# PE order of the paired projections written out, decays loaded behind a part's first level, one tile for three weight sums

## The chip, the cores and the metric

The kernel runs on one core of one Trainium2 chip. The metric is the time of one execution on the device in microseconds (us). The core's engines work in parallel, each through a queue of its own in program order: TensorE (PE, matrix products; PEld are its weight loads), VectorE (DVE), ScalarE (ACT), GpSimd (POOL), and SyncE (SP), which here issues DMA transfers. Semaphores hold an instruction back until what it reads, or what it overwrites, is ready.

## The reference, cut to what matters

128 context tokens and 1024 latent tokens, 1152 in all, go through one layer with D = 1024. The normalised and modulated input h is projected by one weight w_in, and the parts of the projection take different ways:

```python
proj = h @ w_in
q, ff, fb, vi, zA, u, zB, gA, gB = split(proj)
qh = silu(heads(q))                                # 8 heads of 128
log_f, k = forget_gate(ff, lb)                     # f = lb + (1-lb)*sigmoid(ff), k = 1 - f; fb likewise
S_t = diag(f_t) S_(t-1) + k_t v_t^T                # forward in time, and backward with fb
o_t = S_t^T q_t
yA = rms_norm(o_f + o_b) * gnorm_w * silu(zA)
yB = real(fft2(u)) * silu(zB)                      # 4 groups of 128 channels
merged = sigmoid(gA) * (yA @ w_pa) + sigmoid(gB) * (yB @ w_pb)
out = merged @ w_o                                 # then a residual and a norm
```

## The kernel before

The kernel goes through stages: normalisation and the projection of v (to 171 us in the profiled execution), the paired projections (171 to 874 us), the scan of the heads with the branch products (from 874 us) and the output products at the end.

**The paired projections.** `pair(n, evacs)` (L622) projects two column blocks of w_in, 256 columns, for all 1152 tokens by a seven-product scheme (one Strassen step). `PRODUCTS = (1, 5, 6, 2, 7, 4, 3)` is the order of the products. Each has two halves j of 288 tokens, and `mm3` (L205 to L211) makes 12 matmuls of 128x288 of a half: 4 k blocks by 3 terms, since each weight and each input is held as hi + lo (hi*hi L209, lo*hi by L210, hi*lo by L211). So a product has 24 matmuls. Each product has its weights: `raw` (1 MB, two DMAs of 512 KB, L626, one buffer) holds the pair's four blocks; weights 1, 2 and 4 are a block itself, 5, 6 and 3 are sums s1, s2, s2, and 7 is a difference made in raw (L636 on DVE). `split` (L616) makes hi by an ACT cast (L618, wh) and lo by a subtraction (L619, wl: on POOL for 1, 2 and 4, on DVE for the others). Five buffers of hi and lo go round. Products add up in PSUM banks: ACT copies the sums in between to x (L646), DVE or ACT makes the result c (L656, L654), `done` (L659) runs the output's function (silu, sigmoid, forget gate, or nothing) and stores it (L661). Pairs 1 and 2 make u, 3 to 18 the eight heads' q, f, f backward and gate, 19 to 23 the gates, 24 and 25 zB, 26 and 27 gates again.

**Side work.** A generator `four` is stepped from `pair` after some products: first the Fourier transform of u (`fourier`), then `pieces` (L561), which prepares the scan's heads in 16 parts (8 heads, of 640 and 512 tokens each). A part loads its decays f (tile px, L571) and queries q (tile pz, L574), makes kk = 1 - f (ACT, L585, two), qq = q*f (DVE, L586, two) and k0 = the sum of both kk (DVE, L587). Three levels follow, each with 20 or 16 groups of small matmuls 32x32 (`within`, L484), a `merge` into the scores (L475, L477), and, between levels, two ACT copies of halves into the matmuls' operands k0 and q (L470) and a growth of kk, qq and f by the decays (`grow`, DVE, L464 and L466). Behind the second growth it copies f for later (L599), asks for the next part's f (L571), stores kk, qq, f (L602 to L604), and behind the third level asks for the next part's q (L574).

**What sets the order.** A scheduler orders each engine's instructions before the run. Two instructions keep the order in which they are written only where one depends on the other. The helper `matmul` (L201) adds such a dependency between a matmul and the one written before it. The scan stage uses it; the matmuls of `pair` and `within` are plain, so there the scheduler places the levels between a pair's matmuls.

**The start of the scan.** `load_head` (L447) loads a head's kk, qq (1.2 MB each) and fa back. Head 0's loads are made ahead of the last gates, those of heads 1 and 2 at the stage's end.

## Time and profile before

| | us |
|---|---|
| median of 3 runs (lowest, highest) | 1337.24 (1336.79, 1341.56) |
| the profiled execution: its time | 1345.96 |
| the profiled execution: span of the trace | 1344.2 |
| PE busy in the span | 1260.1 (94%) |
| DVE busy | 836.3 (62%) |
| ACT busy | 628.7 (47%) |
| POOL busy | 479.4 (36%) |

The span runs from the first to the last instruction of the trace; the execution's own time is 1.8 us longer. Busy shares are averages over all stages. PE leads by far, so the places count where PE stands still, and the stretches in which the clock granted to it (PEclk, as a share of 2.4 GHz) falls to 0.50, which is 1.2 GHz. A wait is put down to the instruction that released it; "issue" is a wait whose releaser the profile doesn't show.

### The profile page before, as it was taken

How to read it: one execution, taken by the hardware profiler on the slowest of the kernel's cores; microseconds unless marked ns; L12 is line 12 of the kernel's file. 1: busy time of each engine (PE TensorE's matmuls, PEld its weight loads, DVE VectorE, ACT ScalarE, POOL GpSimd, SP SyncE). 2: the span in 40 equal slices, each digit the busy share in tenths (PEclk: the TensorE clock that was granted, in tenths of full speed). 3: DMA queues.
4: the chain of work that ended last, by engine and by line, in shares of the span. 5: the costliest groups of instructions: out<-in, count | busy, mean ns of one | idle time of the engine just before them, and what ended most of it. 6: DMA issues, size and time to landing. Idle time of an engine off the chain costs nothing.

```text
span 1344.2 us, 31219 instructions
## 1 busy us (share of the span) xinstructions
PE 1260.1 (94%) x12768; PEld 1183.8 (88%) x12768; DVE 836.3 (62%) x1391; ACT 628.7 (47%) x1290; POOL 479.4 (36%) x359
## 2 busy tenths in 40 slices
PE   5999989999999989999999999988999889999998
PEld 3679989999998889898899999977899788999886
DVE  7737743434356676675777444485988788565554
ACT  5542233454455655656556444453555444332332
POOL 4515523324412212222112128221432455564563
PEclk7799989999999989999999999998999889999999
DMA  8542223434445546446555634664667754676332
GB/s 314 211 169 65 79 98 116 133 105 149 150 137 183 191 141 230 138 161 204 187 195 186 221 120 153 219 211 153 243 228 237 230 173 131 192 224 211 131 128 95
DMA packets 126162, 229.88 MB, mean 171 GB/s; under 512 B 11441, under 2 KB 78786, under 8 KB 121794
## 3 DMA queue, kind: packets, MB, share of 16 engines
q1 hardware_dynamic: 125730, 226.83, 50.1%
q8 instruction: 100, 1.64, 0.5%
q10 hardware_dynamic: 288, 1.05, 0.3%
q14 instruction: 44, 0.36, 0.1%
HBM read 154.82 MB, written 73.02 MB: 170 GB/s over the span
## 4 chain that ended last, share of the span: by engine, by line
PE 50%; DMA 12%; DVE 10%; issue 5%; ACT 3%; POOL 2%; SPq 1%; DVEq 0%; POOLq 0%; ACTq 0%
PE o_ps L210 7%; PE o_ps L209 7%; PE o_ps L211 7%; PE d_ps L209 5%; PE d_ps L211 5%; PE d_ps L210 5%; DMA raw<-in_w_pr 4%; PE d_ps L200 4%; PE o_ps L200 3%; DMA ya_dr<-gz 2%; DMA wr<-in_w_o 2%; DMA px<-f_dr 1%; PE s_ps L547 1%; DMA yr<-ya_dr 1%; PE s_ps L200 1%
## 5 line engine op out<-in xcount | busy, mean ns | idle before, releaser
L619 POOL TENSOR_TENSOR wl<-raw,wh 128x512 fp32r<-128x512 f32 x81 | 119.5, 1476 | 444.5 <-ACT wh L618 422.3
L619 DVE TENSOR_TENSOR wl<-s,wh 128x512 fp32r<-128x512 f32 x81 | 60.8, 755 | 80.9 <-ACT wh L618 80.7
L186 POOL TENSOR_TENSOR w_lo<-w_raw,w_hi 128x512 fp32r<-128x512 f32 (+1 forms) x36 | 65.0, 1808 | 121.8 <-ACT w_hi L184 121.8
L618 ACT CAST wh<-raw 128x512 fp32r<-128x512 f32 x108 | 66.3, 615 | 71.1 <-DMA raw<-in_w_pr 34.6
L211 PE MATMUL o_ps<-h1h,wl 128*128 128x288 f32 x324 | 98.3, 303 | 0.2 <-POOL wl L619 0.2
L209 PE MATMUL o_ps<-h1h,wh 128*128 128x288 f32 x324 | 97.7, 301 | 0.7 <-ACT wh L618 0.6
L210 PE MATMUL o_ps<-h1l,wh 128*128 128x288 f32 x324 | 97.9, 302 | 0.0
L200 PE MATMUL d_ps<-yh,w_hi 128*128 128x288 f32 x256 | 82.2, 321 | 10.5 <-ACT w_hi L184 5.7
L618 ACT CAST wh<-s 128x512 fp32r<-128x512 f32 x81 | 50.2, 620 | 88.7 <-DVE s L636 26.7
L930 POOL TENSOR_TENSOR merged<-merged,gs 128x288 f32<-128x288 f32 x64 | 64.4, 1018 | 62.5 <-DVE gs L929 59.2
L200 PE MATMUL d_ps<-yh,w_lo 128*128 128x288 f32 x256 | 77.8, 304 | 3.6 <-POOL w_lo L186 3.6
L656 DVE TENSOR_TENSOR c<-o_ps,x 128x288 f32<-128x288 f32 x108 | 47.8, 450 | 53.1 <-PE o_ps L211 43.2
L200 PE MATMUL d_ps<-yl,w_hi 128*128 128x288 f32 x256 | 77.2, 302 | 0.0
L464 DVE TENSOR_TENSOR kk<-kk,fa 128x1152 f32<-128x1152 f32 x40 | 58.9, 1476 | 14.9 <-PE s_ps L200 8.6
L464 DVE TENSOR_TENSOR qq<-qq,fa 128x1152 f32<-128x1152 f32 x40 | 63.7, 1593 | 0.5
L209 PEld LDWEIGHTS o_ps<-h1h,wh 128*128 128x128 f32 x324 | 62.4, 193 | 1.2 <-ACT wh L618 0.8
L211 PEld LDWEIGHTS o_ps<-h1h,wl 128*128 128x128 f32 x324 | 62.3, 192 | 1.1 <-POOL wl L619 0.4
L210 PEld LDWEIGHTS o_ps<-h1l,wh 128*128 128x128 f32 x324 | 62.3, 192 | 0.5 <-issue 0.3
L636 DVE TENSOR_TENSOR s<-raw 128x512 f32<-128x512 f32 x27 | 27.6, 1020 | 55.6 <-DMA raw<-in_w_pr 55.6
L200 PEld LDWEIGHTS d_ps<-yh,w_hi 128*128 128x128 f32 x256 | 50.0, 195 | 12.0 <-ACT w_hi L184 6.1
L586 DVE TENSOR_TENSOR px<-pz,px 128x640 f32<-128x640 f32 (+1 forms) x32 | 23.8, 785 | 53.0 <-DMA px<-f_dr 31.7
L184 ACT CAST w_hi<-w_raw 128x512 fp32r<-128x512 f32 (+1 forms) x48 | 34.8, 725 | 40.6 <-DMA w_raw<-in_w_pab 10.5
(386 smaller groups left out, 4662.9 us busy)
## 6 DMA issues: line engine op xcount, KB each, us to landing
raw<-in_w_pr SPq DMA_DIRECT2D x52, 512.0 KB, 5.5
gs<-g_dr SPq DMA_DIRECT2D x96, 144.0 KB, 3.2
w_raw<-in_w_pab SPq DMA_DIRECT2D x44, 256.0 KB, 3.0
f_dr<-c SPq DMA_DIRECT2D x32, 288.0 KB, 4.3
kk<-kk_dr SPq DMA_DIRECT2D x8, 1152.0 KB, 7.2
qq<-qq_dr SPq DMA_DIRECT2D x8, 1152.0 KB, 7.0
wa<-in_w_ada SPq DMA_DIRECT2D x8, 1024.0 KB
g_dr<-c SPq DMA_DIRECT2D x28, 288.0 KB, 3.8
```

What stands on the lines that cost most here:

```text
L184: nc.scalar.copy(hi, raw)
L186: eng.tensor_tensor(out=lo, in0=raw, in1=hi.bitcast(F32), op=ALU.subtract)
L200: queued(nc.tensor.matmul(*args, **kw))
L209: mm(out, lhsT=sh, rhs=mh, start=first and i == 0, stop=False, **kw)
L210: mm(out, lhsT=sh, rhs=ml, start=False, stop=False, **kw)
L211: mm(out, lhsT=sl_, rhs=mh, start=False, stop=last and i == n - 1, **kw)
L464: nc.vector.tensor_tensor(out=xv, in0=xv, in1=view(ff, off, [[2 * mg, n], [step, 2], [0, m]]), op=ALU.mult)
L618: nc.scalar.copy(hi, src)
L619: eng.tensor_tensor(out=lo, in0=src, in1=hi.bitcast(F32), op=ALU.subtract)
L636: nc.vector.tensor_tensor(out=out, in0=x, in1=y, op=op)
L656: nc.vector.tensor_tensor(out=c[:, h], in0=ps[bank, j], in1=x[i, j], op=ALU.add)
L930: nc.gpsimd.tensor_tensor(out=out, in0=out, in1=gs, op=ALU.add)
```

## The change

1. In `pair` and `within` the matmuls go through `matmul`, so PE runs them in the order in which they are written: a level stands behind the last matmul of the product after which `four` is stepped.
2. The two products qq = q*f of a part move from before its first level to behind the first level's matmuls. The first growth writes the grown decays to a new tile f2 and leaves px's decays alone, the second reads f2, and the fa copy too. The next part's f is asked for behind the first growth.
3. The sums s1 and s2 become one tile `sa`; sums 6 and 3 are made in place.
4. Five empty steps stand between `fourier` and `pieces`, the step behind product 1 of pair 3 goes, and zB comes one pair later (pairs 25 and 26), with one gate pair behind it.
5. The pools sl and sp change places, `km` has one buffer instead of two, and the late v products take their first output tile ahead of their loop.

```diff
@@ -1,5 +1,5 @@
 from contextlib import ExitStack, contextmanager
-from itertools import chain, cycle
+from itertools import chain, cycle, repeat
 
 import numpy as np
 
@@ -48,7 +48,8 @@
 STARTUP = "X0 X1 X2 A0 E0 A1 A2 A3 S0 S1 M0 H0 J0 W0 Q0 R0 S2 M1 J1 I0 W1 H1 Q1 T0 R1 M2 H2 J2 W2 Q2 I1 R2 T1 M3 J3 I2 W3 H3 Q3 R3 T2 M4 H4 J4 I3 Q4 R4 T3 M5 H5 J5 I4 Q5 R5 T4 M6 H6 I5 J6 Q6 R6 T5 M7 H7 J7 Q7 I6 R7 T6 I7 T7"
 PRODUCTS = (1, 5, 6, 2, 7, 4, 3)
 EARLY = (1, 2)
-GATES = 6
+PAUSE = 5
+GATES = 7
 LATE = (4, 8, 16)
 GRAN = 4
 PIECES = ((0, 640), (640, T))
@@ -455,7 +456,7 @@
     def flat(x):
         return x.rearrange("p d t -> p (d t)")
 
-    def grow(ff, kk, qq, m, w=T, g=1):
+    def grow(ff, kk, qq, m, w=T, g=1, into=None):
 
         n, mg, wg = w // (2 * m), m // g, w // g
         dims = [[2 * m, n], [w + m, 2], [1, m]]
@@ -463,7 +464,8 @@
             xv = view(x, 0, dims)
             nc.vector.tensor_tensor(out=xv, in0=xv, in1=view(ff, off, [[2 * mg, n], [step, 2], [0, m]]), op=ALU.mult)
         fv = [view(ff, o, [[wg, 2], [2 * mg, n]]) for o in (0, mg)]
-        nc.vector.tensor_tensor(out=fv[0], in0=fv[0], in1=fv[1], op=ALU.mult)
+        out = fv[0] if into is None else view(into, 0, [[n, 2], [1, n]])
+        nc.vector.tensor_tensor(out=out, in0=fv[0], in1=fv[1], op=ALU.mult)
 
     def halves(x, km, m, w=T):
 
@@ -564,6 +566,7 @@
         x = lp.tile([P, 2, W0], F32, tag="qq", name="px")
         z = lp.tile([P, 2, W0], F32, tag="kk", name="pz")
         sm_ = lp.tile([P, 2, 257], F32, tag="tab", name="ps").rearrange("p a b -> p (a b)")
+        f2 = lp.tile([P, W0 // 2], F32, name="f2")
         todo = [(hd, t0, t1) for hd in range(NH) for t0, t1 in PIECES]
 
         def load_f(hd, t0, t1):
@@ -581,26 +584,32 @@
             a32 = sm_[:, :n * 32].rearrange("p (c t) -> p c t", t=32)
             fa = sm_[:, n * 32:n * 32 + 2 * w // GRAN].rearrange("p (d t) -> p d t", d=2)
             for d in range(2):
-                ds, es = slice(d * w, (d + 1) * w), slice((1 - d) * w, (2 - d) * w)
+                ds = slice(d * w, (d + 1) * w)
                 nc.scalar.activation(kk[:, ds], ff[:, ds], AF.Identity, bias=ones[:, 0:1], scale=-1.0)
-                nc.vector.tensor_tensor(out=qq[:, es], in0=q, in1=ff[:, ds], op=ALU.mult)
             nc.vector.tensor_tensor(out=k0, in0=kk[:, :w], in1=kk[:, w:], op=ALU.add)
             yield
 
             for m, m2 in zip((0,) + EARLY, EARLY + (0,)):
                 ps = scan_ps()
-                within(ps, k0, q, n, nc.tensor.matmul)
+                within(ps, k0, q, n, matmul)
+                if m == 0:
+                    for d in range(2):
+                        ds, es = slice(d * w, (d + 1) * w), slice((1 - d) * w, (2 - d) * w)
+                        nc.vector.tensor_tensor(out=qq[:, es], in0=q, in1=ff[:, ds], op=ALU.mult)
                 merge(a32, m, ps, n)
                 if m2:
                     halves(kk, k0, m2, w)
                     halves(qq, q, m2, w)
-                    grow(ff, kk, qq, m2, w)
-                    if m2 == EARLY[-1]:
-                        nc.scalar.copy(fa, ff.rearrange("p (d t) -> p d t", d=2)[:, :, 0:w:GRAN])
+                    if m == 0:
+                        grow(ff, kk, qq, m2, w, into=f2)
                         if i + 1 < len(todo):
                             load_f(*todo[i + 1])
+                    else:
+                        grow(f2, kk, qq, m2, w, 2)
+                    if m2 == EARLY[-1]:
                         nc.sync.dma_start(kk_dr[hd, :, :, t0:t1], kk.rearrange("p (d t) -> p d t", d=2))
                         nc.sync.dma_start(qq_dr[hd, :, :, t0:t1], qq.rearrange("p (d t) -> p d t", d=2))
+                        nc.scalar.copy(fa, f2[:, :w].rearrange("p (d t) -> p d t", d=2)[:, :, 0:w // 2:GRAN // 2])
                         nc.sync.dma_start(fa_dr[hd, :, :FA].rearrange("p (d t) -> p d t", d=2)[:, :, t0 // GRAN:t1 // GRAN], fa)
                     yield
                 else:
@@ -609,9 +618,9 @@
                     nc.sync.dma_start(fa_dr[hd, :, FA + t0 // P * 32:FA + t1 // P * 32], sm_[:, :n * 32])
         yield
 
-    four = chain(fourier(), pieces())
-
-    with pool("se", 1) as se, pool("sl", 1) as sl_, pool("sp", 1) as sp:
+    four = chain(fourier(), repeat(None, PAUSE), pieces())
+
+    with pool("se", 1) as se, pool("sp", 1) as sp, pool("sl", 1) as sl_:
 
         def split(src, eng):
             hi, lo = (sl_.tile([P, 4, P], F32R, tag=x, name="w" + x, bufs=5) for x in "hl")
@@ -624,15 +633,15 @@
             for d in range(2):
                 ks = slice(4 * d, 4 * d + 4)
                 (nc.scalar if n == 1 else nc.sync).dma_start(raw[:, ks], w_pr[n][:, ks])
-            s1, s2 = (sp.tile([P, 4, P], F32, name=x) for x in ("s1", "s2"))
+            sa = sp.tile([P, 4, P], F32, name="sa")
             (a11, a21), (a12, a22) = [[raw[:, 4 * d:4 * d + 4, i * P:(i + 1) * P] for i in range(2)] for d in range(2)]
 
             def weights(i):
 
                 if i in (1, 2, 4):
                     return split({1: a11, 2: a12, 4: a22}[i], nc.gpsimd)
-                out, x, y, op = {5: (s1, a21, a22, ALU.add), 6: (s2, s1, a11, ALU.subtract),
-                                 7: (a21, a11, a21, ALU.subtract), 3: (s2, a12, s2, ALU.subtract)}[i]
+                out, x, y, op = {5: (sa, a21, a22, ALU.add), 6: (sa, sa, a11, ALU.subtract),
+                                 7: (a21, a11, a21, ALU.subtract), 3: (sa, a12, sa, ALU.subtract)}[i]
                 nc.vector.tensor_tensor(out=out, in0=x, in1=y, op=op)
                 return split(out, nc.vector)
 
@@ -667,7 +676,7 @@
                     if i in (1, 5, 2):
                         ps[bank, j] = any_ps()[:, :SW]
                     mm3(ps[bank, j], [(w[i][0][:, k, :], w[i][1][:, k, :], mov[i][k][0][:, js], mov[i][k][1][:, js])
-                                      for k in range(4)], first=i in (1, 5, 2), skip_group_check=True)
+                                      for k in range(4)], matmul, first=i in (1, 5, 2), skip_group_check=True)
                     if i in (1, 6, 7):
                         keep(i, j)
                     if i == 2:
@@ -680,7 +689,7 @@
                     elif i == 3:
                         result(0, 1, j, 6, "d")
                         done(0, j)
-                if i in (() if n < 3 else (1, 5, 6, 2, 7, 3) if n < 4 else (5, 6, 2, 7, 3) if n < 7 else (6, 7, 3)):
+                if i in (() if n < 3 else (5, 6, 2, 7, 3) if n < 7 else (6, 7, 3)):
                     next(four, None)
 
         def plain(c, j):
@@ -771,7 +780,7 @@
         kk2, qq2 = flat(kk), flat(qq)
         for m in LATE:
             ps = scan_ps()
-            km = s0[0].tile([P, T], F32, name="km", bufs=2)
+            km = s0[0].tile([P, T], F32, name="km")
             halves(kk2, km, m)
             for c in range(NCH):
                 for j in range(4):
@@ -935,6 +944,7 @@
 
     def late_v():
 
+        vos = [s2.tile([P, TW], F32, tag="gz", name="vo", bufs=3)]
         for n, pr in enumerate(LATE_V):
             if n:
                 w = split_v(raws)
@@ -955,7 +965,8 @@
                     mm3(ps, [(*h_at(k, c * P, (c + 1) * P), *w[k]) for k in range(4 * d, 4 * d + 4)], matmul, d == 0, d == 1)
                     if d == 0:
                         yield
-                vo = s2.tile([P, TW], F32, tag="gz", name="vo", bufs=3)[:, :2 * P].rearrange("p (h v) -> p h v", h=2)
+                vo = vos.pop() if vos else s2.tile([P, TW], F32, tag="gz", name="vo", bufs=3)
+                vo = vo[:, :2 * P].rearrange("p (h v) -> p h v", h=2)
                 nc.vector.tensor_copy(vo, ps.rearrange("p (h v) -> p h v", h=2))
                 nc.sync.dma_start(v_dr[2 * pr:2 * pr + 2, :, c, :].rearrange("h p v -> p h v"), vo)
                 yield
```

The first place is PE's queue at the first level of the eighth part (head 3, 512 tokens); o_ps and d_ps are the pair's banks, s_ps that of the level, t2, t3, t1 and h1 inputs of the products. Before:

```order
L210 MATMUL o_ps<-t2l_835,wh 128x288
L211 MATMUL o_ps<-t2h_834,wl 128x288
L209 MATMUL o_ps<-t2h_836,wh 128x288
L210 MATMUL o_ps<-t2l_837,wh 128x288
L211 MATMUL o_ps<-t2h_836,wl 128x288
L484 MATMUL s_ps<-pz 32x32 x16
L209 MATMUL d_ps<-t3h_819,wh 128x288
L210 MATMUL d_ps<-t3l_820,wh 128x288
```

and in the changed kernel:

```order
L201 MATMUL o_ps<-t1h_847,wh 128x288
L201 MATMUL o_ps<-t1l_848,wh 128x288
L201 MATMUL o_ps<-t1h_847,wl 128x288
L201 MATMUL s_ps<-pz 32x32 x16
L201 MATMUL o_ps<-h1h_136,wh 128x288
L201 MATMUL o_ps<-h1l_137,wh 128x288
L201 MATMUL o_ps<-h1h_136,wl 128x288
```

The level stood behind product 7 of a pair, and in other parts behind others or within one; now a part's first level stands behind product 6 (t1) of every pair, its second behind product 7 and its third behind product 3, so that one part goes with one pair (16 parts in 15.6 pairs; before, 16 parts in 13.4).

The second place is a part with 640 tokens: DVE's queue around its k0 sum (L587 before, L589 now) before:

```order
L619 TENSOR_TENSOR wl<-s_6512,wh 128x512
L586 TENSOR_TENSOR px<-pz,px 128x640 x2
L587 TENSOR_TENSOR pz<-pz 128x640
L656 TENSOR_TENSOR c<-o_ps,x_6558 128x288
L636 TENSOR_TENSOR s_6836<-raw 128x512
L656 TENSOR_TENSOR c<-o_ps,x_6573 128x288
L636 TENSOR_TENSOR s_6837<-s_6836,raw 128x512
```

now:

```order
L589 TENSOR_TENSOR pz<-pz 128x640
L628 TENSOR_TENSOR wl<-raw,wh 128x512
L598 TENSOR_TENSOR px<-pz,px 128x640 x2
L628 TENSOR_TENSOR wl<-sa,wh 128x512
L645 TENSOR_TENSOR sa<-raw 128x512
L477 TENSOR_TENSOR ps<-s_ps,m_d 128x160
```

and ACT's queue in the changed kernel, from the fa copy of the part before (L612) over the kk products (L588) to the copies of halves (L472):

```order
L612 COPY ps<-f_4006 128x256
L588 ACTIVATE pz<-px,ones 128x640 x2
L711 ACTIVATE c<-c 128x576
L627 CAST wh<-raw 128x512
L711 ACTIVATE c<-c 128x576
L712 ACTIVATE c<-c,lb,omlb 128x576 x2
L655 COPY x_6701<-d_ps 128x288
L627 CAST wh<-raw 128x512
L655 COPY x_6716<-o_ps 128x288
L627 CAST wh<-sa 128x512
L655 COPY x_6756<-d_ps 128x288
L627 CAST wh<-raw 128x512
```

The two products ahead of k0 went behind it, and behind a weight's lo. On ACT the casts are, in turn, those of weights 7, 4, 3 and, the last one, of weight 1 of the next pair, whose raw DMA has to wait for weight 4's lo and sum 3.

The third place is SP's queue at the start of the scan. Before:

```order
L449 DMA kk<-kk_dr 128x2304
L450 DMA qq<-qq_dr 128x2304
L452 DMA fa<-fa_dr 128x864
L661 DMA g_dr<-c 256x1x288
L818 DMA vt<-v_dr 128x1152
L820 DMA S<-in_state 128x128
L821 DMA S<-in_state 128x128
L661 DMA g_dr<-c 256x1x288 x3
L449 DMA kk<-kk_dr 128x2304
L450 DMA qq<-qq_dr 128x2304
L452 DMA fa<-fa_dr 128x864
L947 DMA raw<-in_w_v 128x512 x4
```

now:

```order
L829 DMA S<-in_state 128x128
L830 DMA S<-in_state 128x128
L670 DMA g_dr<-c 256x1x288 x3
L450 DMA kk<-kk_dr 128x2304
L451 DMA qq<-qq_dr 128x2304
L453 DMA fa<-fa_dr 128x864
L670 DMA g_dr<-c 256x1x288
L450 DMA kk<-kk_dr 128x2304
L451 DMA qq<-qq_dr 128x2304
L453 DMA fa<-fa_dr 128x864
L957 DMA raw<-in_w_v 128x512 x4
```

The first of the two groups of head loads, head 2's, stood seven transfers ahead of head 1's; one transfer is left between the two groups now.

## Rows read from the trace of the kernel before

**Rows 1.** Windows: stretch, length, busy of PE, PEld, DVE, ACT, POOL, PEclk, DMA share, GB/s.

```profile
171.40:389.00 217.60, 217.40 (x1554) 211.12 (x1555) 88.23 (x152) 94.15 (x197) 67.49 (x56) 0.99 0.38 126
389.00:765.00 376.00, 354.60 (x4073) 341.57 (x4073) 255.83 (x398) 223.62 (x398) 80.69 (x52) 0.97 0.54 181
```

**Rows 2.** PE's waits from 389 to 765 us: us in total, times, longest us.

```profile
PE s_ps L484 <- issue: 9.4, 5, 2.2
PE o_ps L209 <- DVE pz L587: 3.7, 1, 3.7
PE o_ps L209 <- DVE c L656: 3.6, 2, 2.2
PE s_ps L484 <- ACT pz L470: 1.9, 2, 1.0
PE d_ps L209 <- DVE c L656: 1.8, 2, 1.0
```

**Rows 3.** Timeline of PE around 562 us: start, us, instruction, [idle before, releaser].

```profile
560.89 0.29 PE L209 MATMUL o_ps<-t2h,wh 128*128 128x288 f32 x1
...
562.36 0.29 PE L211 MATMUL o_ps<-t2h,wl 128*128 128x288 f32 x1
564.90 0.46 PE L484 MATMUL s_ps<-pz 128*32 128x32 f32 x32 [2.25 <-issue]
```

**Rows 4.** Timeline of DVE at the same place.

```profile
562.54 1.29 DVE L586 TENSOR_TENSOR px<-pz,px 128x512 f32<-128x512 f32 x2 [7.06 <-DMA px<-f_dr]
...
564.12 0.68 DVE L587 TENSOR_TENSOR pz<-pz 128x512 f32<-128x512 f32 x1
```

**Rows 5.** Timelines of ACT and of SP's queue at the same place.

```profile
562.49 1.33 ACT L585 ACTIVATE pz<-px,ones 128x512 f32<-128x512 f32 x2 [5.79 <-DMA px<-f_dr]
...
556.45 1.01 SPq L571 DMA_DIRECT2D px<-f_dr  x1
```

**Rows 6.** Windows at half clock, the first and last of five.

```profile
487.60:494.40 6.80, 5.53 (x59) 5.21 (x60) 5.38 (x9) 5.03 (x9) 0.00 (x0) 0.50 0.13 46
...
750.40:753.80 3.40, 3.40 (x16) 3.40 (x15) 3.40 (x7) 2.90 (x6) 0.00 (x0) 0.50 0.00 0
```

**Rows 7.** Groups from 388 to 765 us, by form: busy us, mean ns | idle before.

```profile
L619 POOL TENSOR_TENSOR wl<-raw,wh 128x512 fp32r<-128x512 f32 x43 | 67.3, 1565 | 277.8 <-ACT wh L618 255.7 <-PE o_ps L211 21.9 <-POOL c L696 0.2
...
L618 ACT CAST wh<-raw 128x512 fp32r<-128x512 f32 x56 | 34.2, 612 | 22.5 <-DMA raw<-in_w_pr 17.5 <-PE o_ps L211 4.4 <-PE d_ps L210 0.4
...
L619 DVE TENSOR_TENSOR wl<-s,wh 128x512 fp32r<-128x512 f32 x42 | 28.9, 693 | 17.5 <-ACT wh L618 17.5
...
L484 PE MATMUL s_ps<-pz 128*32 128x32 f32 x1728 | 24.9, 201 | 11.5 <-issue 9.4 <-ACT pz L470 1.9
...
L464 DVE TENSOR_TENSOR pz<-pz,px 128x640 f32<-128x640 f32 x16 | 20.6, 1289 | 4.4 <-ACT pz L470 4.3
...
L703 ACT ACTIVATE c<-c,lb,omlb 128x576 f32<-128x576 f32 x20 | 17.3, 869 | 0.3
...
L646 ACT COPY x<-d_ps 128x288 f32<-128x288 f32 x42 | 16.4, 391 | 3.5 <-PE d_ps L211 3.5
...
L470 ACT COPY pz<-pz 128x640 f32<-128x640 f32 x16 | 14.8, 923 | 1.9 <-PE s_ps L484 1.7
...
L702 ACT ACTIVATE c<-c 128x576 f32<-128x576 f32 x20 | 13.7, 684 | 3.2 <-DVE c L656 2.9
...
L636 DVE TENSOR_TENSOR s<-s,raw 128x512 f32<-128x512 f32 x14 | 9.5, 680 | 0.1
```

**Rows 8.** DMA issues from 389 to 765 us: KB each, median us from issue to landing.

```profile
raw<-in_w_pr SPq DMA_DIRECT2D x28, 512.0 KB, 6.0
...
kk_dr<-pz SPq DMA_DIRECT2D x8, 640.0 KB, 3.4
```

**Rows 9.** The scan's start: the page's DMA issues, and DVE's timeline.

```profile
kk<-kk_dr SPq DMA_DIRECT2D x8, 1152.0 KB, 7.2
...
886.56 1.36 DVE L464 TENSOR_TENSOR kk<-kk,fa 128x1152 f32<-128x1152 f32 x1 [3.79 <-DMA fa<-fa_dr]
```

## The prediction, made before the changed kernel ran

> **What bounds the kernel now.** I read the windows first. In the paired projections before the parts start, PE is busy 217.4 of 217.6 us; in the stretch from 389 to 765 us, where the 16 parts run beside the pairs, 354.6 of 376.0 [rows 1]. So PE is the bound, and what the change can win there is 21.4 us of standing still plus what the clock loses behind the stops. PE's waits in that stretch name the stops [rows 2]: 9.4 us in five waits of a level's small matmuls, released by "issue", 3.7 us for a k0 sum, and three smaller kinds, 3.6, 1.9 and 1.8 us.
>
> "Issue" names no one, so I looked at one place. PE starts its last product matmul at 562.36 and the level at 564.90, 2.25 us idle [rows 3]. On DVE the two qq products start at 562.54, held 7.06 us by the load of f, and the k0 sum, which the level reads, starts at 564.12, runs 0.68 us and ends at 564.80 [rows 4], 0.1 us ahead of the level. So it is the k0 sum again, and in the other four of the five the level also starts 0.1 us behind the end of one. ACT's kk products, which k0 sums, waited 5.79 us for the same load, which SP had issued at 556.45 [rows 5], 6 us earlier. A part in this kernel asks for its f when its predecessor is nearly done, f lands late, the qq products stand ahead of the sum, and the scheduler has put the level where PE has nothing behind it that may pass. These six waits are 9.4 + 3.7 = 13.1 us; one of the two waits of 1.0 us or less for c [rows 2] lies behind a DVE that f held, which makes 14.1.
>
> Then the clock. In five stretches PE's granted clock is 0.50, the lower level of 1.2 GHz: one of 6.8 us and four of 3.4 us [rows 6]; each begins within 3 us of a stop of 1.7 us or more. Half of 20.4 us is lost, 10.2; the four behind k0 waits (6.8 and three of 3.4 us) lose 8.5.
>
> **The change, part by part.** *Decays behind the first level, qq behind k0.* f is asked for behind the first growth instead of the second, some 7 us (two products of 3.2 us) earlier, and into a tile that is free, so it has landed when the part begins. The two qq products, 1.29 us [rows 4], leave the path to k0. Both of the reasons for the six waits go: -14.1 us, and -8.5 us of half clock with them. What is late next is the store of kk, since kk's products overwrite it.
>
> *PE order.* A level now stands behind products 6, 7 and 3 of each pair. The small matmuls are the same 24.9 us in 48 levels, 0.52 each [rows 7]. A product is 24 matmuls at 0.134 us from start to start (11 of them from 560.89 to 562.36 [rows 3]), 3.2 us, a pair 22.4, a pair with a part 24.0. A fixed order has a price of its own: PE can't pass a level, or a product, that isn't ready. The trace before doesn't have that order, so I bound it by the round that one part makes through the queues. Level 1 ends at 5 x 3.2 + 2 x 0.52 = 17.0 us of its pair. Then two copies of halves 1.85, kk's growth 1.29 [rows 7], the store 3.4 [rows 8]: 6.5. Then, in ACT's order, the next kk (1.33 us for 512 tokens [rows 5], 1.6 for 640), two sigmoids 1.37, the cast of weight 7 0.61, two scalings 1.74, a copy x 0.39, the cast of weight 4 0.61: 6.4. Its lo on POOL takes 1.57, and then raw is free; the next raw takes 6.0 to land [rows 8] and weight 1's cast 0.61, x 0.39: 8.6. Behind these stand halves 1.85, the casts of 5 and 6 (0.61 each), the first lo 0.69 and the sum 0.68 between them, and two copies x 0.78: 5.2 [rows 7]. In all 26.7, some 27 with the issue of a DMA; PE wants the last x, product 7's second half, at product 4's second half, 24.0 - 17.0 + 5 x 3.2 + 1.04 + 1.6 = 25.6 after level 1. So a part with scalings comes 1.1 to 1.6 us late. But a stop in one pair comes behind its level 1, so the next pair starts later by as much and is late by less: in a steady state half of it, some 0.8 us. The nine head pairs (10 to 18) have scalings; the seven gate and zB pairs have none, 1.74 us less, and are in time. I take 9 x 0.8 = +7 us. The ends are 0 and, with all 16 pairs late by the whole 1.6, 25 us.
>
> *One tile for the sums.* Sum 6 has to wait for the cast and the lo of weight 5, 0.61 + 0.69 [rows 7], in each of 27 pairs. In a pair without a part ACT and DVE are idle over half of the time [rows 1], and five buffers of weights run ahead; beside a part it is in the round above. Alone 0; 27 x 1.3 = 35 us if no lead were left.
>
> *Start of the scan.* Head 2's loads are now directly ahead of head 1's, 2.8 MB more in front. kk's alone takes 7.2 us, and DVE already waits 3.79 us for head 1's decays [rows 9]. Head 1's first growth comes later by 0 to 10 us. Part of it lies beside the matmuls of late v: I take +3, with ends 0 and 6.
>
> *The rest.* The empty steps start the parts at pair 9.4 as before (9.6); zB a pair later has no reader before the scan; `km` with one buffer is overwritten behind a growth that waits for the same matmuls anyway; the pools' places and the late v tile change addresses. Head 0's loads come a pair before their use; 7.2 us [rows 9] are covered by 22.4. Each 0, and 2 us for the lot if the covers fail.
>
> **The sum.** -14.1 - 8.5 + 7 + 3 = -12.6 us on the profiled execution, whose own time is 1345.96: 1333.4. That execution lies 8.7 us above the median of the runs, 1337.24, so the median becomes 1324.6: **1325 us**, 0.9% faster. About 0.5%, 6.7 us, can be told from no change.
>
> **The rivals.** *Whole gain.* If raw lands early enough the round is short enough everywhere, all 21.4 + 10.2 us go, and nothing comes back: 1337 - 32 = 1305 us. For it speaks that a fixed order also lets the casts stand where the weights are wanted; against it that raw takes 6.0 us in this stretch [rows 8]. The Trainium skill, "DMA: Bandwidth & Descriptors", section "Anatomy of one DMA — SWDGE (gpsimd) path", gives a fit of 2.0 us plus the bytes by 436 GB/s, an estimate of 3.2 us for 512 KB; by it the round would be under 25 us and this rival the forecast. The row of 6.0 us, on SP's queue with other transfers beside, speaks against it. Lower end 1305.
>
> *The round binds, slower.* If raw, waiting behind stores of the part, lands 2 us later than the median, or the sum of weight 6 has no lead, then a pair is late by 1.6 us or more in all 16 pairs: +25 us, and the clock falls behind many such stops as it did behind those of 1.7 us or more: half of a 3.4 us stretch [rows 6] in 16 pairs is 27 us; with half of them 14. Then -22.6 + 25 + 14 + 3 = +19: 1356 us. The point from which it decides is a mean pair of 26 us beside parts, where the kernel before has 23.5 us a part with its stops. For it speaks that ACT and DVE wait in line for raw already (17.5 us at weight 1's cast [rows 7]); against it that a part now has three products between levels to catch up in. The Trainium skill, "Trainium Kernel Development and Optimization", Best Practices, says to double-buffer; the change takes a buffer away from the sums. No row of the kernel before shows what that costs by itself.
>
> *It only moves.* The k0 waits go and the same amount comes back at the x copies and casts, below the stops that cost clock: -14 - 8 + 15 to 20 + 3, within 4 us of no change: 1336 us.
>
> **How the numbers follow.** Chances: the forecast 0.52 (its own range 1314 to 1334 by the ends of its terms), whole gain 0.13, it only moves 0.14, the round binds 0.21. The forecast's upper end and the third case lie within 0.5%. Faster by over 0.5%: 0.52 x 0.92 + 0.13 = 0.61; within: 0.18; slower: 0.21. The range goes from 1305 to 1350, which leaves out the upper half of the slow case.
>
> **What would show it.** Right: no wait of a level (s_ps) above 0.5 us in the stretch with the parts, kk's products on ACT held by the store of kk and not by f's load, at most two stretches at 0.50, small waits of product 4's or 7's matmuls for ACT's x in the head pairs and none in the gate pairs, and a longer wait of DVE for head 1's decays. Wrong: waits of PE for wh or x of 1.5 us and more in each pair (the round binds), or level waits as before.

## The result, and the profile after

The changed kernel took 1324.51 us (median of 4 runs, 1321.07 to 1326.95), the kernel before, beside it, 1337.01: a ratio of 0.9896, 95% interval 0.9869 to 0.9922. It is about 1% faster; 1325 had been forecast. The profiled execution took 1325.72 us, 20.2 less than that of before, where the medians differ by 12.5.

Windows of the changed kernel (columns as in [rows 1]); the second holds all 16 parts, which now end 17 us later:

```profile
168.40:389.00 220.60, 219.81 (x1571) 213.55 (x1572) 91.35 (x155) 95.92 (x200) 66.70 (x56) 0.99 0.39 128
389.00:790.00 401.00, 393.87 (x4439) 382.10 (x4439) 275.84 (x427) 239.56 (x438) 84.06 (x58) 1.00 0.56 186
```

PE stands still for 7.1 of 401 us, where it was 21.4 of 376 [rows 1], and its granted clock is 1.00. From the first pair to the last the stage takes 681.9 us (168.5 to 850.4) instead of 702.2 (171.4 to 873.7): all of the 20.2. (Ahead of the stage it gains 3.0 us, behind it, in the branch products, it loses 3.1.) Of the stage's gain 11.7 us are less standing still of PE, and 8.7 are less busy time (680.1 to 671.5 us for the same matmuls), in which the half-clock stretches count. PE's waits from 168 to 851 us answer to [rows 2]:

```profile
PE o_ps L201 <- ACT x L655: 6.0, 8, 1.4
PE d_ps L201 <- DVE vo L407: 4.3, 1, 4.3
PE s_ps L201 <- DMA pz<-q_dr: 2.7, 1, 2.7
PE d_ps L201 <- ACT x L655: 1.5, 2, 0.8
```

No level waits for k0 or for halves any more, and no product for c. The wait for vo lies ahead of the stage, and before had one too. New are 7.5 us for copies x (0.6 before) and one wait of the first level for its q. ACT's waits for what its kk products need, from 389 to 790 us, against the 5.79 us for f in [rows 5]:

```profile
ACT pz L588 <- DMA kk_dr<-pz: 4.9, 7, 2.0
...
ACT pz L588 <- DMA px<-f_dr: 0.5, 1, 0.5
```

f is there; the store of kk holds them, shortly. And the issues of raw in the same stretch, 6.0 us in [rows 8]:

```profile
raw<-in_w_pr SPq DMA_DIRECT2D x32, 512.0 KB, 3.3
```

Half of a raw block (512 KB) lands in 3.3 us. Both medians are of few transfers, since the trace shows the landing of seven of these 32 and of six of the 28 before. The casts of weight 1 that waited for raw start 3.3 to 5.1 us behind its issue here (ten of them) and 4.0 to 7.0 us before (ten), so raw does come sooner, but by less than the medians say; why it does is not shown. The Trainium skill, "DMA: Bandwidth & Descriptors", section "Anatomy of one DMA — SWDGE (gpsimd) path", gives, for transfers that gpsimd issues, a fit that makes an estimate of 3.2 us for 512 KB. The 3.3 us of this trace agree with it and the 6.0 of before don't, both on SP's queue.

One of the new stops, which ends at 526.55 us. First PE, then SP, ACT and DVE in the changed kernel's timelines:

```profile
526.55 0.40 PE L201 MATMUL o_ps<-t3h,wh 128*128 128x288 f32 x1 [1.42 <-ACT x L655]
```

```profile
513.82 0.82 SPq L635 DMA_DIRECT2D raw<-in_w_pr  x2
```

```profile
518.08 0.62 ACT L627 CAST wh<-raw 128x512 fp32r<-128x512 f32 x1 [3.27 <-DMA raw<-in_w_pr]
...
525.59 0.62 ACT L627 CAST wh<-sa 128x512 fp32r<-128x512 f32 x1 [3.79 <-DVE sa L645]
526.11 0.39 ACT L655 COPY x<-o_ps 128x288 f32<-128x288 f32 x1
```

```profile
519.51 1.12 DVE L645 TENSOR_TENSOR sa<-raw 128x512 f32<-128x512 f32 x1 [4.57 <-DMA raw<-in_w_pr]
...
521.35 1.14 DVE L465 TENSOR_TENSOR pz<-pz,px 128x512 f32<-128x512 f32 x1
522.34 1.17 DVE L465 TENSOR_TENSOR px<-px 128x512 f32<-128x512 f32 x1
523.36 0.79 DVE L665 TENSOR_TENSOR c<-o_ps,x 128x288 f32<-128x288 f32 x2
524.08 0.67 DVE L628 TENSOR_TENSOR wl<-sa,wh 128x512 fp32r<-128x512 f32 x1
524.78 0.69 DVE L645 TENSOR_TENSOR sa<-sa,raw 128x512 f32<-128x512 f32 x1
```

Product 4's second half waits for the last x, the copy for the cast of weight 6 ahead of it on ACT, that for sum 6, which stands on DVE behind lo 5, which stands behind the growths. ACT waited 3.27 us for raw, as foretold for this place.

### The profile page after: what moved, and what is told of

The parts are those of the page before. It is cut to its first block, busy times and chain, and to the rows that moved or that the text cites. A ratio compares the mean times of both kernels' runs of the same rounds, so it can differ in the third digit from the quotient of the medians.

```text
span 1323.9 us, 31278 instructions
## 1 busy us (share of the span) xinstructions
PE 1246.3 (94%) x12768; PEld 1172.0 (89%) x12768; DVE 843.2 (64%) x1391; ACT 624.4 (47%) x1290; POOL 475.3 (36%) x359
## 5 line engine op out<-in xcount | busy, mean ns | idle before, releaser
L628 POOL TENSOR_TENSOR wl<-raw,wh 128x512 fp32r<-128x512 f32 x81 | 114.7, 1416 | 449.6 <-ACT wh L627 448.1
L627 ACT CAST wh<-sa 128x512 fp32r<-128x512 f32 x81 | 50.3, 621 | 130.3 <-DVE sa L645 58.4
L628 DVE TENSOR_TENSOR wl<-sa,wh 128x512 fp32r<-128x512 f32 x81 | 60.2, 743 | 73.9 <-ACT wh L627 73.5
L645 DVE TENSOR_TENSOR sa<-raw 128x512 f32<-128x512 f32 x27 | 31.0, 1149 | 85.0 <-DMA raw<-in_w_pr 85.0
L939 POOL TENSOR_TENSOR merged<-merged,gs 128x288 f32<-128x288 f32 x64 | 61.1, 968 | 58.5 <-DVE gs L938 58.0
L465 DVE TENSOR_TENSOR qq<-qq,fa 128x1152 f32<-128x1152 f32 x40 | 67.6, 1691 | 1.6 <-PE s_ps L201 1.4
L655 ACT COPY x<-d_ps 128x288 f32<-128x288 f32 x81 | 32.1, 396 | 61.0 <-PE d_ps L201 60.9
L201 PEld LDWEIGHTS d_ps<-yh,w_lo 128*128 128x128 f32 x256 | 50.0, 195 | 4.9 <-POOL w_lo L187 4.9
```

Of the source, the lines that this page charges most:

```text
L201: queued(nc.tensor.matmul(*args, **kw))
L465: nc.vector.tensor_tensor(out=xv, in0=xv, in1=view(ff, off, [[2 * mg, n], [step, 2], [0, m]]), op=ALU.mult)
L627: nc.scalar.copy(hi, src)
L628: eng.tensor_tensor(out=lo, in0=src, in1=hi.bitcast(F32), op=ALU.subtract)
L645: nc.vector.tensor_tensor(out=out, in0=x, in1=y, op=op)
L655: nc.scalar.copy(x[i, j], ps["a", j])
```

## The experiments

Each ratio is to runs of the kernel before, made on the same chip.

**1. The order alone.** Edit, on the kernel before:

```diff
-                within(ps, k0, q, n, nc.tensor.matmul)
+                within(ps, k0, q, n, matmul)
...
-                                      for k in range(4)], first=i in (1, 5, 2), skip_group_check=True)
+                                      for k in range(4)], matmul, first=i in (1, 5, 2), skip_group_check=True)
```

> The kernel before, with the PE order fixed and nothing else. Theory (order and early decays need each other): the level sits 9.6 us into its pair, so the k0 waits go even with late decays, but ACT now holds the copies and casts of the next pair behind kk products that wait for f, to about 7 us into the pair; raw comes free late and product 7 and 4 wait for x some 3 us a pair: 1350 to 1385 us, slower than before. Rival (the order carries the gain alone): 1322 to 1330 us.

1370.94 us, ratio 1.024 (1.0192 to 1.0288): slower, within the range of the theory. PE's waits in its pair stage:

```profile
PE o_ps L200 <- ACT x L646: 17.1, 14, 2.0
PE s_ps L200 <- DVE pz L587: 9.4, 1, 9.4
PE s_ps L547 <- DMA tab<-in_seq_dft: 7.5, 3, 2.9
...
PE s_ps L508 <- DMA cu<-u_dr: 5.6, 1, 5.6
PE o_ps L200 <- DVE c L656: 5.2, 9, 1.2
```

The 17.1 us for x lie at product 6's second half, not at products 7 and 4 as the theory has it: the copy of product 1 that it waits for stands on ACT right behind kk products that waited for f (2.1 us at 507.8 us). That is a shorter way than the ring through raw. And 22.5 us (9.4, 7.5 and 5.6) stand between 342 and 379 us, at the end of the Fourier part and at the first level, and the clock is at half for another 23.9 us from 360 us on: the steps as listed ask for Fourier tables and the first part too early for a fixed order. The theory hadn't foreseen that share, so its range was met in part by luck.

**2. All but the order.** The two lines of experiment 1 undone on the changed kernel:

```diff
-                within(ps, k0, q, n, matmul)
+                within(ps, k0, q, n, nc.tensor.matmul)
...
-                                      for k in range(4)], matmul, first=i in (1, 5, 2), skip_group_check=True)
+                                      for k in range(4)], first=i in (1, 5, 2), skip_group_check=True)
```

> The changed kernel with the PE order left to the scheduler, all other edits kept. Theory: decays are there early, so no level waits for k0 by more than 0.5 us, but the scheduler puts levels within products and some waits of 1 to 2 us stay: 1326 to 1334 us. Rival (the order carries the gain): 1334 to 1345 us, the k0 waits and half-clock stretches of before are back.

1327.59 us, ratio 0.9911 (0.9876 to 0.9946). No wait for k0 is left and no half-clock stretch between 173 and 869 us. What stays is as the theory has it:

```profile
PE o_ps L210 <- DVE c L665: 6.6, 5, 2.1
```

The stage takes 679.7 us, 681.9 in the changed kernel. The order adds nothing to early decays that this can tell from 0.9896.

**3. Decays asked for later.** The lines of `load_f` moved behind the second growth:

```diff
-                        if i + 1 < len(todo):
-                            load_f(*todo[i + 1])
                     else:
                         grow(f2, kk, qq, m2, w, 2)
+                        if i + 1 < len(todo):
+                            load_f(*todo[i + 1])
```

> The changed kernel, f of the next part asked for behind the second growth instead of the first. Theory: kk's products wait for f, which lands about 2.5 us later than the store of kk; half of it shows as PE waits for x in each of 16 pairs: +15 to +25 us, 1340 to 1350. Rival (the store of kk holds kk's products anyway, or the pair has room): 0 to +3 us.

1325.25 us, ratio 0.9898 (0.9864 to 0.9932). It tells nothing: SP's queue shows f's load 4.4 us ahead of kk's store (578.43 and 582.82) as in the changed kernel (573.73 and 578.12). So the load went by what it depends on, the first growth, and not by the line. Experiment 6 does it properly.

**4. qq ahead of k0 again.** The two products moved back, and the lines behind the level taken out:

```diff
+                es = slice((1 - d) * w, (2 - d) * w)
                 nc.scalar.activation(kk[:, ds], ff[:, ds], AF.Identity, bias=ones[:, 0:1], scale=-1.0)
+                nc.vector.tensor_tensor(out=qq[:, es], in0=q, in1=ff[:, ds], op=ALU.mult)
...
-                if m == 0:
-                    for d in range(2):
...
-                        nc.vector.tensor_tensor(out=qq[:, es], in0=q, in1=ff[:, ds], op=ALU.mult)
```

> The changed kernel with both qq products again ahead of the k0 sum. Theory: a level 0 that stands behind product 6 has about 6 us of room for 1.3 to 1.6 us of qq products: 0 to +3 us, 1323 to 1329. Rival (the shorter path to k0 is what took the waits away): +10 to +15 us, with waits of the level for k0 in the trace.

1324.29 us, ratio 0.9892 (0.9862 to 0.9923): no difference. With f there in time, and the level behind product 6, the longer path to k0 costs nothing.

**5. Early decays alone.** On the kernel before: the tile f2, the early load, qq behind level 0, one tile for the sums, and one buffer of km to make room. Order, steps and zB as before. The new lines are those of the change's own diff for `grow`, `pieces` and `sa`, save that `within` keeps plain matmuls (the first two lines, against the changed kernel), and `km` (the other two, against the kernel before):

```diff
-                within(ps, k0, q, n, matmul)
+                within(ps, k0, q, n, nc.tensor.matmul)
...
-            km = s0[0].tile([P, T], F32, name="km", bufs=2)
+            km = s0[0].tile([P, T], F32, name="km")
```

> The kernel before with the second and third edit (decays loaded behind the first growth into the freed tile, qq behind k0, one tile for the sums) and the single km that makes room; the PE order stays the scheduler's, and the steps and zB stay. Theory (the early decays carry the gain): no wait for k0, no half-clock stretch behind one, 1320 to 1330 us. Rival (they need the fixed order, the pause or the later zB): 1333 to 1340.

1328.78 us, ratio 0.9951 (0.9926 to 0.9975). Half of the gain, at the upper end of the theory's range. No wait for k0; its stage takes 686.9 us, with 10.2 us of waits for x and c and one stretch of 6.8 us at half clock.

**6. No early decays.** The changed kernel with f2 undone: the decays grow in place, and f is asked for behind the fa copy.

```diff
-                        grow(ff, kk, qq, m2, w, into=f2)
-                        if i + 1 < len(todo):
-                            load_f(*todo[i + 1])
+                        grow(ff, kk, qq, m2, w)
                     else:
-                        grow(f2, kk, qq, m2, w, 2)
+                        grow(ff, kk, qq, m2, w)
...
+                        nc.scalar.copy(fa, ff.rearrange("p (d t) -> p d t", d=2)[:, :, 0:w:GRAN])
+                        if i + 1 < len(todo):
+                            load_f(*todo[i + 1])
...
-                        nc.scalar.copy(fa, f2[:, :w].rearrange("p (d t) -> p d t", d=2)[:, :, 0:w // 2:GRAN // 2])
```

> The changed kernel without the tile for the grown decays: they grow in place, f of the next part is asked for behind the second growth and the copy of it. Here the load moves in SP's queue, which it did not in the run with the load written later. Theory: kk's products wait for f on ACT, x copies come late, PE's waits for x go from 7.5 to 20 us or more: 1335 to 1345 us. Rival (the store of kk holds them as long): 0 to +3 us.

1358.91 us, ratio 1.0173 (1.0138 to 1.0207): worse than the theory's 1345. PE's wait for x, and ACT's for f:

```profile
PE o_ps L201 <- ACT x L655: 28.1, 14, 3.4
```

```profile
ACT pz L588 <- DMA px<-f_dr: 26.6, 16, 3.5
```

This has the size and the place of the prediction's slower rival: 22.2 of the 28.1 us lie at product 4's second half, and five stretches of 3.4 us are at half clock. The way in is another one. Raw's median to land is 3.4 us, as in the changed kernel, but kk's products hold ACT, raw comes free late, x comes late. There is no wait for k0 here: in the fixed order the late load shows as waits for x instead.

**7. Order, steps, pause and zB, no more.** Experiment 1, and

```diff
-GATES = 6
+PAUSE = 5
+GATES = 7
...
-    four = chain(fourier(), pieces())
+    four = chain(fourier(), repeat(None, PAUSE), pieces())
...
-                if i in (() if n < 3 else (1, 5, 6, 2, 7, 3) if n < 4 else (5, 6, 2, 7, 3) if n < 7 else (6, 7, 3)):
+                if i in (() if n < 3 else (5, 6, 2, 7, 3) if n < 7 else (6, 7, 3)):
```

> The kernel before with the fixed PE order, the pause, the shorter list of steps and the later zB. Theory (the order alone lost most of its time by starting parts before their inputs were there): the 9.4 us wait for k0 and the waits for the Fourier tables go, x waits of some 17 us stay: 1335 to 1347 us. Rival (the order itself is the loss while decays are late): 1355 us or more.

1350.06 us, ratio 1.0121 (1.0078 to 1.0164), between theory and rival. The waits at the start of the parts fall to one of 3.7 us for q and the 23.9 us at half clock are gone; 19.0 us for x (17.7 and 1.3, the 17.7 again at product 6's second half) and 5.7 for c stay.

**8. Sum 6 made in raw.** Sum 6 equals a22 minus weight 7's difference, and raw's first block is free by then, so it needs no lo 5 to be done.

```diff
+                if i == 6:
+                    nc.vector.tensor_tensor(out=a21, in0=a11, in1=a21, op=ALU.subtract)
-                out, x, y, op = {5: (sa, a21, a22, ALU.add), 6: (sa, sa, a11, ALU.subtract),
-                                 7: (a21, a11, a21, ALU.subtract), 3: (sa, a12, sa, ALU.subtract)}[i]
+                out, x, y, op = {5: (sa, a21, a22, ALU.add), 6: (a11, a22, a21, ALU.subtract),
+                                 7: (a21, None, None, None), 3: (sa, a12, a11, ALU.subtract)}[i]
-                nc.vector.tensor_tensor(out=out, in0=x, in1=y, op=op)
+                if i != 7:
+                    nc.vector.tensor_tensor(out=out, in0=x, in1=y, op=op)
```

> The changed kernel, with the sum of weight 6 made in raw's free first block as a22 minus weight 7's difference, so that it doesn't wait for weight 5's lo in the common tile. Theory (the common tile sets the stops at product 4: raw lands, sum 5, growths, c results, lo 5, sum 6, cast 6, copy x): the x waits of 7.5 us fall below 2, 1316 to 1320 us. Rival (the late landing of raw or ACT's line sets them): 1323 to 1327 us.

1323.36 us, ratio 0.9908 (0.9883 to 0.9933): no difference. In the trace the waits for x fall to 4.4 us in three and the stage takes 678.9 us, 3.0 less than in the changed kernel, which the ratio can't tell. The waits of the zB and gate pairs are gone, but two of 1.8 us are left, in pairs where the changed kernel has 1.4 us and none. At the one of 529 us, POOL, SP and ACT show:

```profile
513.78 1.43 POOL L708 TENSOR_TENSOR c<-c,sg 128x576 f32<-128x576 f32 x1 [4.17 <-ACT sg L706]
516.01 1.64 POOL L708 TENSOR_TENSOR c<-c,sg 128x576 f32<-128x576 f32 x1 [0.80 <-ACT sg L706]
517.61 1.74 POOL L628 TENSOR_TENSOR wl<-raw,wh 128x512 fp32r<-128x512 f32 x1
```

```profile
519.37 0.81 SPq L635 DMA_DIRECT2D raw<-in_w_pr  x2
```

```profile
523.71 0.62 ACT L627 CAST wh<-raw 128x512 fp32r<-128x512 f32 x1 [4.75 <-DMA raw<-in_w_pr]
```

Two silu products stand on POOL ahead of lo 4, raw's last reader there; raw goes out right behind it. The common tile was one link of the ring. That POOL's products are the next one is not shown: experiment 11 moves them and is slower.

**9. The pools of before.** On the changed kernel:

```diff
-    with pool("se", 1) as se, pool("sp", 1) as sp, pool("sl", 1) as sl_:
+    with pool("se", 1) as se, pool("sl", 1) as sl_, pool("sp", 1) as sp:
```

> The changed kernel with the pools in the order of before, which puts head 2's loads ahead of the late weights' transfers and the stores of the last gates again, away from head 1's. Theory of the prediction (the loads ahead of head 1's cost 3 us): DVE's wait for head 1's decays falls, 1320 to 1323 us. Rival (that wait is covered by late v and head 0's matmuls, as the trace after hints, since from the last pair to the first branch product it takes 60 us as before): 1323 to 1327, no difference.

1321.35 us, ratio 0.9880 (0.9849 to 0.9912). DVE's wait for head 1's decays is 0.60 us here (first row), 4.33 in the changed kernel (second), where the row of [rows 9] was 3.79:

```profile
867.19 1.36 DVE L465 TENSOR_TENSOR kk<-kk,fa 128x1152 f32<-128x1152 f32 x1 [0.60 <-DMA fa<-fa_dr]
```

```profile
869.03 1.36 DVE L465 TENSOR_TENSOR kk<-kk,fa 128x1152 f32<-128x1152 f32 x1 [4.33 <-DMA fa<-fa_dr]
```

PE's wait for vo behind it falls from 2.4 to 0.2 us, and from the last pair to the first branch product it takes 58.8 us instead of 60.1. That is 1.3 us in the trace, too little for the ratios to show.

**10. An earlier end of the Fourier part.** On the changed kernel:

```diff
-PAUSE = 5
+PAUSE = 6
...
-                if i in (() if n < 3 else (5, 6, 2, 7, 3) if n < 7 else (6, 7, 3)):
+                if i in (() if n < 3 else (1, 5, 6, 2, 7, 3) if n < 4 else (5, 6, 2, 7, 3) if n < 7 else (6, 7, 3)):
```

> The changed kernel with six empty steps and the step behind product 1 of pair 3 kept: the parts stand where they stand, but the Fourier part ends one product earlier, so its store, whose landing the first q load waits for, goes earlier. Theory: PE's wait of 2.7 us (2.7 to 4.0 in the runs) for the first part's q goes, and the half-clock stretch behind it where there was one: 1319 to 1323 us. Rival (q lands late for raw's transfer beside it): no difference.

1322.45 us, ratio 0.9888 (0.9860 to 0.9917). PE's 2.7 us for the first q are gone; its stage takes 680.4 us, 1.5 less. The ratio can't tell that.

**11. Experiment 8 with the silu product of the q pairs on DVE.** The zB pairs use the same line.

```diff
-                nc.gpsimd.tensor_tensor(out=c, in0=c, in1=sg, op=ALU.mult)
+                nc.vector.tensor_tensor(out=c, in0=c, in1=sg, op=ALU.mult)
```

> The run with sum 6 made in raw, and with it the q pairs' silu product on DVE instead of POOL, where it stood ahead of weight 4's lo, the last reader of raw. Theory (the x waits that were left, 4.4 us in three, are raw landing late behind that lo): x waits below 1.5 us, 1318 to 1321 us. Rival (DVE's two products of a q pair put off its own sums and growths by as much): 1322 to 1326 us.

1339.02 us, ratio 1.0014 (0.9991 to 1.0036), some 15 us slower than experiment 8, and neither theory nor rival had that size. Its waits for x:

```profile
PE o_ps L201 <- ACT x L658: 8.8, 8, 1.5
PE d_ps L201 <- ACT x L658: 8.4, 6, 4.4
```

17.2 us instead of 4.4, 12.2 of them in four head pairs and 5.0 in the zB pairs. At one of the head pairs POOL, DVE and SP show:

```profile
571.11 1.29 POOL L628 TENSOR_TENSOR wl<-raw,wh 128x512 fp32r<-128x512 f32 x1 [6.26 <-ACT wh L627]
```

```profile
573.48 0.75 DVE L708 TENSOR_TENSOR c<-c,sg 128x576 f32<-128x576 f32 x1
```

```profile
569.62 5.14 SPq L673 DMA_DIRECT2D q_dr<-c  x2
574.86 1.07 SPq L635 DMA_DIRECT2D raw<-in_w_pr  x2
```

POOL is done with raw at 572.40. But the second silu product now stands on DVE behind the two qq products and ends at 574.23, the store of q waits for it, and raw stands behind that store in SP's queue: it goes out 2.5 us after POOL has let it go. From 389 to 860 us SP's stores wait so in five places:

```profile
SPq L673 <- DVE c L708: 18.9, 5, 4.0
```

What makes the waits of the zB pairs stays open.

**12. Experiments 8, 9 and 10 together**, their three diffs on the changed kernel.

> The changed kernel with three of the edits tried: sum 6 in raw, the earlier Fourier end with six empty steps, and the pools of before. Theory (each takes away a stop of its own: x copies some 3 us, the first q load 2.7 us with its clock, a µs or two at the scan's start): 1316 to 1320 us, a ratio to before of 0.984 to 0.987. Rival (a stop that goes leaves the next transfer to be waited for, as in the run with sum 6 in raw alone): 1320 to 1324, a ratio of 0.988 to 0.991.

1322.29 us, ratio 0.9875 (0.9852 to 0.9899). The time lies in the rival's range, the ratio between the two ranges, and the interval reaches into both; that the waits for x are 7.2 us again speaks for the rival. It beats the kernel before, and no interval sets it apart from the changed one.

## Why the prediction was right

*The waits for k0* (-14.1 us): all six gone, and with them the other 6.3 us of [rows 2], which the sum had kept. *The half clock* (-8.5): all of the 10.2 us went, since the fifth stretch, behind a wait that the sum had left alone, went too. That the early decays are the cause is shown from both sides: without them the changed kernel is 1.7% slower than before (experiment 6), with them and without the fixed order it is 0.9% faster (experiment 2), and alone, but for the qq products, the one tile of the sums and the single km that go with them, 0.5% (experiment 5). So they carry about half of the gain by themselves; for the rest only experiments with more of the change speak.

The prediction laid all six waits on the load of f, from a look at one. In two of them, at 537.1 and 748.9 us, kk was ready before, and the qq products that stood ahead of k0 waited for q. DVE before:

```profile
534.71 1.56 DVE L586 TENSOR_TENSOR px<-pz,px 128x640 f32<-128x640 f32 x2 [3.91 <-DMA pz<-q_dr]
...
746.90 1.29 DVE L586 TENSOR_TENSOR px<-pz,px 128x512 f32<-128x512 f32 x2 [5.93 <-DMA pz<-q_dr]
```

ACT's kk products ended at 534.94 and 745.50, 1.3 and 2.7 us ahead of these. So the second reason, the place of the qq products, counted there. In the fixed order it costs nothing (experiment 4); no run puts them behind k0 in the kernel before and changes nothing else.

*The fixed order* (+7, ends 0 and 25): the ring is real and its place was the one foretold, product 4's second half, waiting for x. Five pairs with parts wait 0.5 to 1.4 us there, 4.4 in all, not nine by 0.8; two of the five are gate pairs, said to have none. The two zB pairs add 2.6, the first of them with three 576 KB loads of yf ahead of raw in SP's queue, an early pair 0.6, and the first part 2.7 for its q, which wasn't in the sum. Together 10.2 in place of 7.

That the size came out so near is in part luck. The round that ends in the stop shown above begins behind level 1, the second of the three, of the part before; first PE, then ACT:

```profile
498.54 0.56 PE L201 MATMUL s_ps<-pz 128*32 128x32 f32 x40
```

```profile
508.14 1.34 ACT L588 ACTIVATE pz<-px,ones 128x512 f32<-128x512 f32 x2 [1.29 <-DMA kk_dr<-pz]
...
510.76 0.62 ACT L627 CAST wh<-raw 128x512 fp32r<-128x512 f32 x1
```

To the last x it takes 27.4 us, 26.7 in the prediction, but in other pieces: from level 1 to the start of kk 9.0 us (6.5 in the sum), from there to the end of weight 4's cast 3.2 (6.4), from there over lo 4, raw and weight 1's cast to its copy 7.6 (8.6), and from there to the last x 7.5 (5.2), since DVE has growths and results c ahead of lo 5 and sum 6. With the 3.3 us that raw has now in place of 6.0, the prediction's own pieces make less than the 25.6 us that PE gives them, and no stop. With late decays the ring reaches its upper end: experiment 6 has 22.2 us at this place, so the end of 25 was not idle.

*The start of the scan* (+3): the mechanism is there. Head 1's first growth stands 18.7 us behind the end of the last pair, 12.9 before and 15.1 in experiment 9. But it is worth about 1.3 us (experiment 9), and against before it shows nothing: 60.2 us from the last pair to the first branch product then, 60.1 now. The profiled execution loses 3.1 us elsewhere, in the branch products (303.9 to 306.9 us); other runs with the same order there have 302.6 to 303.8 (experiments 3, 4 and 10), so I don't lay it on the change.

*The sum* of -12.6 us was too small for the profiled executions, which differ by 20.2, and agrees with the medians' 12.5. So the term that carried the profiled execution's 8.7 us over the median unchanged to the new kernel was wrong: the profiled execution after lies 1.2 us over its median. The underrated gain and this offset cancelled, so that the forecast hit the median by luck to half a us; what the prediction had right is which stops go and where new ones come. Its forecast's own range, 1314 to 1334, is also narrower than the ends of its terms, which make 1346 at the upper end. Runs of before spread from 1331 to 1345 us in these comparisons, and it stays open which of its stops came and went, since only one execution of it has a trace.

*The rivals.* The whole gain did not come: 10.2 us of stops are back. The rival in which the round binds is the fate of this kernel without early decays. The Trainium skill, "Trainium Kernel Development and Optimization", Best Practices, says to double-buffer so that DMA overlaps with compute. That giving up one of the two tiles of the sums costs time, no run shows here: experiment 8 takes the wait at the common tile away, and the ratio stays.

Open: which of the steps, the pause, the later zB and the pools make the difference between experiments 5 and 2 (0.9951 and 0.9911, whose intervals overlap).

## What to carry to other kernels

When a profile says "issue", look at what ended just before the instruction started, and follow that to its load: here five nameless waits and one named one were all waits for one sum, four with the load of f behind them and two with that of q, so look at more than one. Fixing an engine's order was worth nothing measurable here by itself, and went with a loss of 1.2 to 2.4% where what it waits for was late (experiments 1, 6 and 7): first make the inputs early, by freeing their buffer earlier, then fix the order. And of a sum made against one execution, ask which of its stops other executions have before its offset to the median is carried over.

## What was not expected

Moving a load in the source left it where it was in its queue (experiment 3): what counts is what it depends on. One elementwise product of 128x576, twice in each q pair and also in the zB pairs, moved from POOL to DVE cost some 15 us over experiment 8 (experiment 11), at the head pairs through a store that stood ahead of a load in SP's queue. And the same 512 KB transfer has a median of 6.0 us or 3.3 to land (six and seven landings), in the same stage with nearly the same DMA share (0.54 and 0.56).
